# Attention steps that carry gate products: a reordering of a two-layer mixing kernel

## The chip, the cores and the metric

The kernel runs on one core of a Trainium2 chip. The metric is the device time of one execution in microseconds, lower is better. The time before is the median of three runs; one more execution was taken with the hardware profiler, and every row below is from that one.

## The reference, cut to what matters

Two layers of a backbone over 256 latent and 256 context tokens, width 1024. In the second layer only the latent tokens are carried to the end.

```python
for l in range(DEPTH):
    x, s = ffn_sublayer(x, ...), ffn_sublayer(s, ...)
    ...
    out_x, out_s, v_first = token_mixing(hx, hs, p, v_first, ..., not last)
    x = x + mod_x[:, :, 5] * out_x
    x = ffn_sublayer(x, ...)

def token_mixing(hx, hs, p, ...):
    cols_x, cols_s = split_cols(hx @ p['w_in'], IN_SPLITS), split_cols(hs @ p['w_in'], IN_SPLITS)
    ...
    ret_x  = retention_output(ox_f + flip_seq(ox_b), cols_x[3])
    att_x  = window_context_attention(aqx, akx, avx, aks, avs, sink)
    rwkv_x = rwkv_output(yx_f + yx_b, r_x, v_x, dirs_x, g_x, p)
    out_x  = branch_merge(ret_x, att_x, rwkv_x, cols_x[8], p)

def branch_merge(ret, att, rw, gate_logits, p):
    g_ret, g_att, g_rw = jnp.split(jax.nn.sigmoid(gate_logits), N_BRANCH, axis=-1)
    merged = g_ret * (ret @ p['w_ret']) + g_att * (att @ p['w_att']) + g_rw * (rw @ p['w_rwkv'])
    return merged @ p['w_out']
```

The gates are `cols_x[8]`: 3072 columns of the projection, 24 tiles of 128. They need nothing but the normed input, and nothing needs them before the branches are merged.

## The kernel before, in words

Activations lie with features on the partitions and the 512 tokens (context, then latent) along a row. A weight block is 128x128; four of them come in one DMA (`raw`, queue SP), ScalarE casts them to a high part (`whi`, line 114) and VectorE makes the rest (`wlo`, line 115). A product of a block with a tile of activations is three matmuls (`mm3`, lines 186 to 188). `dense` (line 330) does one output tile of 128 columns: eight blocks, 24 matmuls, 512 wide in layer 0 and 256 wide in layer 1, where only the latent half is wanted.

`mix` (its loop stands near the end of the listing) runs the token mixing of a layer as a list of pieces named in `ORDER` (line 55), one string for each layer:

- `lo`, `c0` to `c3`: the projections of the third branch (RWKV-7), four head pairs.
- `A`p and `C`p: `rw_front` of pair p for the context half (`A`) and the latent half (`C`). It ends in matmuls at line 976, in VectorE work on their results, in a trip through DRAM, and in a triangular solve on GpSimd, 31 rounds of two operations (lines 1008 and 1009), whose result goes to DRAM (`td`).
- `B`p and `D`p: `rw_back` of the same. `rw_merge` loads the solve's result (`z`), copies it on ScalarE (line 1026) and transposes it on VectorE (lines 1023 and 1027), and uses it in small matmuls (lines 1035 and 1040). `rw_chain` then walks four chunks in two directions; each step is a chain of matmul 1079/1081, ScalarE 1083, matmul 1086, ScalarE 1088, matmul 1090, VectorE 1102, and on to the next 1079/1081. `rw_out` closes it (1131, 1134).
- `P`, `H`: projections and heads of the retention branch. `kv`, `q0`, `q1`: keys, values and queries of attention.
- `t0` to `t3`: `att_pair`, two heads of attention each, over blocks of 128 queries (four steps in layer 0, two in layer 1). A step has for each of its two heads the scores (lines 757, 758, 761, one PSUM bank `ps_sc`), the maximum on VectorE (764), the exponential on ScalarE (767), transposes on TensorE (773), a copy on ScalarE (774) and the products with the values (776).
- `G0` to `G11`: `gates`, two gate tiles each: `dense`, a tanh on ScalarE (line 589), a store to DRAM.

After the list, `branches` projects and merges the three branches with the stored gates. The list is the order of tracing, not the order on the engines: the program is scheduled by the framework with a timeline of its own, which lets a later piece fill the waits of an earlier one, within the buffers that are free. `plan_mix` (line 58) packs the weights in the order of the list.

Of the kernel before, what the change touches and what calls it, by code (L numbers as in the profile page):

```python
# [51 lines left out]

ORDER = ['lo c0 A0 C0 B0 P0 kv c1 D0 H0 H1 q0 A1 t0 P1 t1 G0 C1 B1 H2 G1 c2 H3 G2 D1 A2 G3 q1 B2 P2 G4 C2 H4 t2 G5 t3 c3 A3 G6 H5 D2 G7 G8 P3 H6 G9 C3 B3 H7 D3 G10 G11', 'lo c0 A0 C0 P0 H0 kv B0 D0 c1 A1 H1 q0 t0 G0 t1 C1 G1 B1 P1 c2 D1 H2 A2 H3 P2 C2 G2 G3 H4 G4 c3 q1 G5 t2 t3 G6 B2 H5 D2 G7 A3 C3 G8 P3 B3 G9 G10 H6 H7 D3 G11']


def plan_mix(l):
    r0 = RCOL // 128
    out = []  # L60
    for w in ORDER[l].split():
        k, j = w[0], w[1:]
        if w == "lo":
            out.append(("lo", [("mix", kt, r0 + 12 + j) for kt in range(KT) for j in range(3)]))
            if l > 0:
                out.append(("vd", [("vd", 0, 0), ("vd", 0, 1)]))
        elif k == "c":
            p = int(j)
            out += [(f"r{p}", fm("mix", r0 + p)), (f"k{p}", fm("mix", r0 + 4 + p)), (f"v{p}", fm("mix", r0 + 8 + p))]
        elif k == "P":  # L70
            p = int(j)
            out += [(f"rq{p}", fm("mix", p)), (f"rk{p}", fm("mix", 4 + p)), (f"rv{p}", grp("mix", 8 + 2 * p))]
        elif k == "H":
            out.append((f"rg{j}", fm("mix", 16 + int(j))))
        elif w == "kv":
            out.append(("akv", grp("mix", 28)))
        elif k == "q":
            out.append((f"aq{j}", grp("mix", 24 + 2 * int(j))))
        elif k == "G":
            out += [(f"g{g}", fm("mix", 45 + g)) for g in range(2 * int(j), 2 * int(j) + 2)]  # L80
    for n in range(KT):
        out.append((f"ba{n}", fm("watt", n, 4)))
    out += [(f"br{n}", fm("wret", n)) for n in range(KT)]
    out += [(f"bw{n}", fm("wrw", n, 4)) for n in range(KT)]
    out += [(f"wo{n}", fm("wout", n)) for n in range(KT)]
    return out
# [36 lines left out]
def body(nc, tc, I, O, es, dbg=None):  # L123
# [61 lines left out]
    def mm3(o, w, h, start, stop):  # L185
        PE.matmul(o, w[0], h[0], start=start, stop=False)  # L186
        PE.matmul(o, w[0], h[1], start=False, stop=False)  # L187
        PE.matmul(o, w[1], h[0], start=False, stop=stop)  # L188

    def rsqrt(y, x):  # L190
        p, n = x.shape
# [138 lines left out]
    def dense(W, key, H, c, o):  # L330
        bl = W.take(key)
        for j, t in enumerate(bl):
            mm3(o[:, c], W.get(t), hl(H[j], c), j == 0, j == len(bl) - 1)

    def last_out(W, key, H, gate):

# [243 lines left out]
        SP.dma_start(out=st["od"][8 + h, :, c], in_=g[:, c])  # L580


    def gates(W, H, j, S, st):
        c = span(S)
        for g in range(2 * j, 2 * j + 2):
            o = ps("mm")
            dense(W, f"g{g}", H, c, o)
            t = ft()
            A.activation(t[:, c], o[:, c], AF.Tanh, scale=0.5)
            SP.dma_start(out=st["gd"][g, :, c], in_=t[:, c])  # L590

    def spilled(st, j, n, S, dst, mark, scale=None):
        c = span(S)
# [145 lines left out]
                    V.tensor_sub(qT[pr][h][ot, CS[half]], pt[hs, pr * 256:pr * 256 + 256], qT[pr][h][hs, CS[half]].bitcast(F32))  # L739
        st["qT", 2 * grp_], st["qT", 2 * grp_ + 1] = qT  # L740

    def att_pair(pj, S, st):
        c = span(S)
        q = st["qT", pj]
        (kd, kl), v = st["kT"], st["v"]
        t0 = c.start // 128
        po = ps("po")
        nm, es, sum_ = (sm(8, k, 4).rearrange("p (t h) -> p t h", h=2) for k in ("anm", "aes", "asum"))
        for qt in range(t0, 4):
            qs = slice(qt * 128, qt * 128 + 128)  # L750
            n = 256 if qt < 2 else 512
            nk = n // 128
            sc, p = [], []
            for hh in range(2):
                sc.append(ps("sc")[:, 0:n])
                p.append(mk([128, 512], "ae", 4)[:, 0:n])
                PE.matmul(sc[hh], q[hh][:, qs], kd[hh][:, 0:n], start=True, stop=False)
                PE.matmul(sc[hh], q[hh][:, qs], kl[hh][:, 0:n], start=False, stop=(qt < 2))
                if qt >= 2:
                    far = 5 - qt  # L760
                    PE.matmul(sc[hh][:, 256 + (far - 2) * 128:256 + (far - 2) * 128 + 128], st["aeye"], st["amask"][:, qt - 2], start=False, stop=True)
            mx = sm(2, "amx", 16)
            for hh in range(2):
                V.tensor_reduce(mx[:, hh:hh + 1], sc[hh], axis=AX.X, op=ALU.max)
                V.scalar_tensor_tensor(nm[:, qt, hh:hh + 1], mx[:, hh:hh + 1], -1.0, st["nsink"][:, 2 * pj + hh:2 * pj + hh + 1], ALU.mult, ALU.min)
            for hh in range(2):
                A.activation(p[hh], sc[hh], AF.Exp, bias=nm[:, qt, hh:hh + 1], accum_out=sum_[:, qt, hh:hh + 1])
            for hh in range(2):
                if hh == 0 or n == 512:
                    pt, pT = ps("ap"), mk([128, 512], "aT", 2)  # L770
                w0 = hh * 256 if n == 256 else 0
                for j in range(nk):
                    PE.transpose(pt[:, w0 + j * 128:w0 + j * 128 + 128], p[hh][:, j * 128:j * 128 + 128], ident)
                A.copy(pT[:, w0:w0 + n], pt[:, w0:w0 + n])
                for j in range(nk):
                    PE.matmul(po[:, qt * 128 + hh * 64:qt * 128 + hh * 64 + 64], pT[:, w0 + j * 128:w0 + j * 128 + 128], v[:, j * 128 + hh * 64:j * 128 + hh * 64 + 64], start=(j == 0), stop=(j == nk - 1))
        nt = slice(t0, 4)
        V.tensor_tensor(es[:, nt], nm[:, nt], st["sink"][:, 2 * pj:2 * pj + 2].unsqueeze(1).to_broadcast([128, 4 - t0, 2]), ALU.add)
        A.activation(es[:, nt], es[:, nt], AF.Exp)
        V.tensor_tensor(sum_[:, nt], sum_[:, nt], es[:, nt], ALU.add)  # L780
        V.reciprocal(sum_[:, nt], sum_[:, nt])
        y, t = mk([128, 512], "ae", 4), mk([128, 512], "aT", 2)
        V.tensor_tensor(y[:, c].rearrange("p (u d) -> p u d", d=64), po[:, c].rearrange("p (u d) -> p u d", d=64),
                        sum_[:, nt].rearrange("p t h -> p (t h)").unsqueeze(2).to_broadcast([128, 2 * (4 - t0), 64]), ALU.mult)
        yt = ps("ap")
        for qt in range(t0, 4):
            PE.transpose(yt[:, qt * 128:qt * 128 + 128], y[:, qt * 128:qt * 128 + 128], ident)
        A.copy(t[:, c], yt[:, c])
        SP.dma_start(out=st["od"][4 + pj, :, c], in_=t[:, c])
# [386 lines left out]
    def mix(l, W, H, S, vf, mark, st):  # L1176
# [4 lines left out]
        for w in ORDER[l].split():  # L1181
# [15 lines left out]
            elif k == "q":  # L1197
                att_q(W, H, int(j), S, st)
            elif k == "t":
                att_pair(int(j), S, st)  # L1200
            elif k == "G":
                gates(W, H, int(j), S, st)
        return branches(W, S, st), st["mark"]

    def mix_out(l, W, ms, S, xd):
# [161 lines left out]
```

## Time and profile before

| | |
|---|---|
| median of 3 runs | 2948.22 us (2942.67 to 2951.27) |
| the profiled execution's own time | 2950.47 us |
| its span in the profile | 2948.7 us |
| TensorE (PE) busy | 2797.0 us, 95% |
| VectorE (DVE) busy | 2002.5 us, 68% |
| ScalarE (ACT) busy | 1319.8 us, 45% |
| GpSimd (POOL) busy | 376.2 us, 13% |
| mean granted clock of TensorE | 0.963 |

The mixing of layer 0 takes the stretch from about 410 to 1314 us, that of layer 1 from about 2070 to 2747 us; the rest is feed-forward, which the change does not touch. Matmuls overlap in the records, so a matmul's own duration is longer than the time it adds; the time it adds is read from one start to the next. [...] In the timeline a bracket holds the idle time of that engine just before the row and what ended it.

### The profile page before, as it was taken

The page shows a single profiled execution, that of the slowest core. Times are in us where ns is not written, and L with a number is a line of the kernel's source. Part 1 is how long each engine was busy: PE and PEld are TensorE (multiplying, and loading weights), DVE is VectorE, ACT ScalarE, POOL GpSimd, SP SyncE. Part 2 cuts the span into 40 slices and gives each one's busy share as a digit, 9 for nine tenths or more (in the row PEclk, how much of TensorE's full clock was granted, in tenths as well). Part 3 has the DMA queues.
Part 4 walks back from the last instruction along what each step waited for, and adds up shares of the span by engine and source line. Part 5 has one row for each costly group of instructions (what it writes and reads, how often), then busy time and mean ns, then how long its engine had stood idle before and what let it go on. Part 6 is the DMA issues. An engine that isn't in the chain of part 4 may idle for free. (4 is left out here: it accounts for less than half of the span.)

```text
span 2948.7 us, 47410 instructions
## 1 busy us (share of the span) xinstructions
PE 2797.0 (95%) x16761; PEld 2389.1 (81%) x16761; DVE 2002.5 (68%) x4677; ACT 1319.8 (45%) x2968; POOL 376.2 (13%) x1068
## 2 busy tenths in 40 slices
PE   7999999889999999999999999999989889899999
PEld 6888888767877787788888888888878788788999
DVE  7977668676676666566756466465787767678655
ACT  3322245556555654333223232233567665565544
POOL 0000000522132112000000000000033434330000
PEclk9999999789999999999999999999999888899999
DMA  7655534212333136534534435343433234246554
GB/s 267 232 189 183 163 122 130 83 39 82 111 97 89 49 123 207 176 102 147 195 114 169 147 111 185 104 164 122 137 90 108 75 110 116 61 124 212 170 179 154
DMA packets 259727, 400.97 MB, mean 136 GB/s; under 512 B 78752, under 2 KB 96288, under 8 KB 259488
## 3 DMA queue, kind: packets, MB, share of 16 engines
q1 hardware_dynamic: 259488, 397.93, 42.2%
q8 instruction: 132, 2.16, 0.3%
q14 instruction: 107, 0.88, 0.1%
HBM read 368.33 MB, written 25.82 MB: 134 GB/s over the span
## 5 line engine op out<-in xcount | busy, mean ns | idle before, releaser
L114 ACT CAST whi<-raw 128x512 fp32r<-128x512 f32 x954 | 564.1, 618 | 675.7 <-PE ps_mm L187 350.0
L186 PE MATMUL ps_mm<-hall,whi 128*128 128x512 f32 (+1 forms) x2320 | 845.1, 365 | 10.2 <-DVE rr_v L801 4.0
L188 PE MATMUL ps_mm<-hall,wlo 128*128 128x512 f32 (+1 forms) x2320 | 842.6, 364 | 2.0 <-DVE wlo L115 2.0
L187 PE MATMUL ps_mm<-hall,whi 128*128 128x512 f32 (+1 forms) x2320 | 840.8, 363 | 0.0
L115 DVE TENSOR_TENSOR wlo<-raw,whi 128x512 fp32r<-128x512 f32 x954 | 643.8, 691 | 104.3 <-ACT whi L114 68.3
L186 PEld LDWEIGHTS ps_mm<-hall,whi 128*128 128x128 f32 x2320 | 442.9, 191 | 80.6 <-ACT cst L981 4.4
L188 PEld LDWEIGHTS ps_mm<-hall,wlo 128*128 128x128 f32 x2320 | 441.6, 191 | 74.8 <-DVE wlo L115 4.1
L187 PEld LDWEIGHTS ps_mm<-hall,whi 128*128 128x128 f32 x2320 | 442.0, 191 | 71.4 <-issue 0.2
L186 PE MATMUL ps_mm<-hid,whi 128*128 128x512 f32 (+1 forms) x737 | 260.6, 354 | 0.0
L187 PE MATMUL ps_mm<-hid,whi 128*128 128x512 f32 (+1 forms) x737 | 259.9, 354 | 0.0
L188 PE MATMUL ps_mm<-hid,wlo 128*128 128x512 f32 (+1 forms) x737 | 257.3, 354 | 0.0
L1008 POOL TENSOR_TENSOR cst<-acc,cst 128x60 f32<-128x60 f32 (+24 forms) x496 | 172.4, 348 | 615.5 <-DMA acc<-ad__10934 59.2
L401 DVE TENSOR_TENSOR ft<-ft,ps_mm 128x512 f32<-128x512 f32 (+1 forms) x80 | 49.7, 621 | 210.4 <-PE ps_mm L188 198.1
L373 DVE SCALAR_TENSOR_TENSOR x<-ps_mm,cst,x 128x256 f32<-128x256 f32 x136 | 61.0, 480 | 193.1 <-PE ps_mm L188 193.1
L853 POOL TENSOR_TENSOR ll<-lora,lh 128x512 fp32r<-128x512 f32 x8 | 10.3, 1282 | 1359.2 <-DVE ft L300 942.6
L1009 POOL TENSOR_TENSOR cst<-cst 128x60 f32<-128x60 f32 (+24 forms) x496 | 176.2, 355 | 38.1
L236 DVE SCALAR_TENSOR_TENSOR ft<-m,cd 128x1024 bf16<-128x1024 f32 x136 | 163.0, 1221 | 9.8 <-DMA m<-ada 9.8
L237 DVE SCALAR_TENSOR_TENSOR m<-m,cd 128x1024 f32<-128x1024 f32 x136 | 165.4, 1221 | 0.7
L186 PEld LDWEIGHTS ps_mm<-hid,whi 128*128 128x128 f32 x737 | 139.1, 189 | 19.6
L187 PEld LDWEIGHTS ps_mm<-hid,whi 128*128 128x128 f32 x737 | 139.1, 189 | 19.4
L188 PEld LDWEIGHTS ps_mm<-hid,wlo 128*128 128x128 f32 x737 | 138.5, 189 | 19.4
L187 PE MATMUL ps_mm<-wlo,hall 128*128 128x256 f32 x416 | 122.6, 295 | 2.7 <-DVE wlo L115 2.6
(339 smaller groups left out, 4505.3 us busy)
## 6 DMA issues: line engine op xcount, KB each, us to landing
m<-ada SPq DMA_DIRECT2D x136, 512.0 KB, 4.4
raw<-w0b SPq DMA_DIRECT2D x214, 256.0 KB, 2.9
raw<-w1b SPq DMA_DIRECT2D x211, 256.0 KB, 3.2
raw<-w0a SPq DMA_DIRECT2D x132, 256.0 KB, 2.8
raw<-w0c SPq DMA_DIRECT2D x132, 256.0 KB, 4.5
raw<-w1a SPq DMA_DIRECT2D x132, 256.0 KB, 4.3
raw<-w1c SPq DMA_DIRECT2D x132, 256.0 KB, 3.9
gd<-ft SPq DMA_DIRECT2D x24, 256.0 KB, 2.0
```

Of the source, the lines that this page charges most:

```text
L114: nc.scalar.copy(hi, raw)
L115: nc.vector.tensor_sub(lo, raw, hi.bitcast(F32))
L186: PE.matmul(o, w[0], h[0], start=start, stop=False)
L187: PE.matmul(o, w[0], h[1], start=False, stop=False)
L188: PE.matmul(o, w[1], h[0], start=False, stop=stop)
L236: V.scalar_tensor_tensor(junk, raw, 1.0, st["cond"][0], ALU.mult, ALU.mult, accum_out=md[:, kt, 0:1])
L237: V.scalar_tensor_tensor(raw, raw, 1.0, st["cond"][1], ALU.mult, ALU.mult, accum_out=md[:, kt, 1:2])
L373: V.scalar_tensor_tensor(xs[n][:, CS[s]], o[:, CS[s]], gate[:, n, s:s + 1], xs[n][:, CS[s]], ALU.mult, ALU.add)
L401: V.tensor_tensor(sg[:, c], sg[:, c], pu[:, c], ALU.mult)
L853: G.tensor_sub(ll, lw, lh.bitcast(F32))
L1008: G.tensor_tensor(w, acc[j // 16][:, j % 16, j + 1:32].unsqueeze(1).to_broadcast([128, m, n]), tt[:, 0:m, j:j + 1].to_broadcast([128, m, n ...
L1009: G.tensor_tensor(tt[:, 0:m, j + 1:32], tt[:, 0:m, j + 1:32], w, ALU.add)
```

## The change

In the list the pieces `G0` to `G7` are gone from both layers, and `P`, `q1`, `t` and their neighbours stand closer or in another order; `G8` to `G11`, the last eight gate tiles, are kept at their places. The sixteen other gate tiles are done inside attention: pair j computes gates 4j to 4j+3, one in each step in layer 0 and two in each step in layer 1, traced after the step's exponentials. Two orders are forced on TensorE (`issue_after` adds an order on the engine of the instruction, not a wait on a semaphore): the gate's matmuls come after the last score matmul of the step, and the step's transposes come after the gate's last matmul. `mm3` and `dense` return their last instruction for this. The program has the same instructions on every engine as before, in another order.

```diff
@@ -52,7 +52,7 @@
 
 
 
-ORDER = ['lo c0 A0 C0 B0 P0 kv c1 D0 H0 H1 q0 A1 t0 P1 t1 G0 C1 B1 H2 G1 c2 H3 G2 D1 A2 G3 q1 B2 P2 G4 C2 H4 t2 G5 t3 c3 A3 G6 H5 D2 G7 G8 P3 H6 G9 C3 B3 H7 D3 G10 G11', 'lo c0 A0 C0 P0 H0 kv B0 D0 c1 A1 H1 q0 t0 G0 t1 C1 G1 B1 P1 c2 D1 H2 A2 H3 P2 C2 G2 G3 H4 G4 c3 q1 G5 t2 t3 G6 B2 H5 D2 G7 A3 C3 G8 P3 B3 G9 G10 H6 H7 D3 G11']
+ORDER = ['lo c0 A0 C0 B0 P0 kv c1 D0 H0 H1 q0 A1 t0 P1 C1 t1 B1 H2 c2 H3 D1 A2 q1 B2 t2 P2 C2 H4 c3 t3 A3 H5 D2 G8 P3 H6 G9 C3 B3 H7 D3 G10 G11', 'lo c0 A0 C0 P0 H0 kv B0 D0 c1 A1 H1 q0 t0 C1 t1 B1 P1 c2 D1 H2 A2 H3 P2 C2 H4 c3 q1 t2 B2 t3 H5 D2 A3 C3 G8 P3 B3 G9 G10 H6 H7 D3 G11']
 
 
 def plan_mix(l):
@@ -76,8 +76,9 @@
             out.append(("akv", grp("mix", 28)))
         elif k == "q":
             out.append((f"aq{j}", grp("mix", 24 + 2 * int(j))))
-        elif k == "G":
-            out += [(f"g{g}", fm("mix", 45 + g)) for g in range(2 * int(j), 2 * int(j) + 2)]
+        elif k in "Gt":
+            n = 2 if k == "G" else 4
+            out += [(f"g{g}", fm("mix", 45 + g)) for g in range(n * int(j), n * int(j) + n)]
     for n in range(KT):
         out.append((f"ba{n}", fm("watt", n, 4)))
     out += [(f"br{n}", fm("wret", n)) for n in range(KT)]
@@ -185,7 +186,7 @@
     def mm3(o, w, h, start, stop):
         PE.matmul(o, w[0], h[0], start=start, stop=False)
         PE.matmul(o, w[0], h[1], start=False, stop=False)
-        PE.matmul(o, w[1], h[0], start=False, stop=stop)
+        return PE.matmul(o, w[1], h[0], start=False, stop=stop).ins
 
     def rsqrt(y, x):
         p, n = x.shape
@@ -330,7 +331,8 @@
     def dense(W, key, H, c, o):
         bl = W.take(key)
         for j, t in enumerate(bl):
-            mm3(o[:, c], W.get(t), hl(H[j], c), j == 0, j == len(bl) - 1)
+            ins = mm3(o[:, c], W.get(t), hl(H[j], c), j == 0, j == len(bl) - 1)
+        return ins
 
     def last_out(W, key, H, gate):
 
@@ -580,14 +582,15 @@
         SP.dma_start(out=st["od"][8 + h, :, c], in_=g[:, c])
 
 
-    def gates(W, H, j, S, st):
+    def gates(W, H, gs, S, st):
         c = span(S)
-        for g in range(2 * j, 2 * j + 2):
+        for g in gs:
             o = ps("mm")
-            dense(W, f"g{g}", H, c, o)
+            ins = dense(W, f"g{g}", H, c, o)
             t = ft()
             A.activation(t[:, c], o[:, c], AF.Tanh, scale=0.5)
             SP.dma_start(out=st["gd"][g, :, c], in_=t[:, c])
+        return ins
 
     def spilled(st, j, n, S, dst, mark, scale=None):
         c = span(S)
@@ -739,7 +742,7 @@
                     V.tensor_sub(qT[pr][h][ot, CS[half]], pt[hs, pr * 256:pr * 256 + 256], qT[pr][h][hs, CS[half]].bitcast(F32))
         st["qT", 2 * grp_], st["qT", 2 * grp_ + 1] = qT
 
-    def att_pair(pj, S, st):
+    def att_pair(W, H, pj, S, st):
         c = span(S)
         q = st["qT", pj]
         (kd, kl), v = st["kT"], st["v"]
@@ -755,22 +758,27 @@
                 sc.append(ps("sc")[:, 0:n])
                 p.append(mk([128, 512], "ae", 4)[:, 0:n])
                 PE.matmul(sc[hh], q[hh][:, qs], kd[hh][:, 0:n], start=True, stop=False)
-                PE.matmul(sc[hh], q[hh][:, qs], kl[hh][:, 0:n], start=False, stop=(qt < 2))
+                mark = PE.matmul(sc[hh], q[hh][:, qs], kl[hh][:, 0:n], start=False, stop=(qt < 2)).ins
                 if qt >= 2:
                     far = 5 - qt
-                    PE.matmul(sc[hh][:, 256 + (far - 2) * 128:256 + (far - 2) * 128 + 128], st["aeye"], st["amask"][:, qt - 2], start=False, stop=True)
+                    mark = PE.matmul(sc[hh][:, 256 + (far - 2) * 128:256 + (far - 2) * 128 + 128], st["aeye"], st["amask"][:, qt - 2], start=False, stop=True).ins
             mx = sm(2, "amx", 16)
             for hh in range(2):
                 V.tensor_reduce(mx[:, hh:hh + 1], sc[hh], axis=AX.X, op=ALU.max)
                 V.scalar_tensor_tensor(nm[:, qt, hh:hh + 1], mx[:, hh:hh + 1], -1.0, st["nsink"][:, 2 * pj + hh:2 * pj + hh + 1], ALU.mult, ALU.min)
             for hh in range(2):
                 A.activation(p[hh], sc[hh], AF.Exp, bias=nm[:, qt, hh:hh + 1], accum_out=sum_[:, qt, hh:hh + 1])
+
+            ng = 4 // (4 - t0)
+            with tc.issue_after(mark):
+                mark = gates(W, H, range(4 * pj + (qt - t0) * ng, 4 * pj + (qt - t0 + 1) * ng), S, st)
             for hh in range(2):
                 if hh == 0 or n == 512:
                     pt, pT = ps("ap"), mk([128, 512], "aT", 2)
                 w0 = hh * 256 if n == 256 else 0
                 for j in range(nk):
-                    PE.transpose(pt[:, w0 + j * 128:w0 + j * 128 + 128], p[hh][:, j * 128:j * 128 + 128], ident)
+                    with tc.issue_after(mark):
+                        PE.transpose(pt[:, w0 + j * 128:w0 + j * 128 + 128], p[hh][:, j * 128:j * 128 + 128], ident)
                 A.copy(pT[:, w0:w0 + n], pt[:, w0:w0 + n])
                 for j in range(nk):
                     PE.matmul(po[:, qt * 128 + hh * 64:qt * 128 + hh * 64 + 64], pT[:, w0 + j * 128:w0 + j * 128 + 128], v[:, j * 128 + hh * 64:j * 128 + hh * 64 + 64], start=(j == 0), stop=(j == nk - 1))
@@ -1197,9 +1205,9 @@
             elif k == "q":
                 att_q(W, H, int(j), S, st)
             elif k == "t":
-                att_pair(int(j), S, st)
+                att_pair(W, H, int(j), S, st)
             elif k == "G":
-                gates(W, H, int(j), S, st)
+                gates(W, H, range(2 * int(j), 2 * int(j) + 2), S, st)
         return branches(W, S, st), st["mark"]
 
     def mix_out(l, W, ms, S, xd):
```

What the scheduler made of it is shown at three places. Lines of the changed kernel are numbered a few higher: 186 to 188 became 187 to 189, 757/758/761 became 760/761/764, 773 became 781, 774 became 782, 776 became 784, 589 became 591, and the lines of the RWKV branch moved by 8 (1026 became 1034, 1079 became 1087).

**TensorE, layer 0, one step of pair 1 (`t1`).** Before, transposes of one head, then the next head's scores, then other pieces' small matmuls, then the product with the values:

```order
L773 MATMUL ps_ap<-cst,ae 128x128 x4
L757 MATMUL ps_sc<-kd,qT 128x512
L758 MATMUL ps_sc<-kl,qT 128x512
L761 LDWEIGHTS pa
L761 MATMUL ps_sc<-pa 128x128
L1052 MATMUL ps_rx<-cst,rr_v 128x128 x2
L1040 MATMUL ps_rx<-tg,rb 32x32 x9
L776 MATMUL ps_po<-kv,aT 128x64 x4
```

In the changed program, a step of pair 1:

```order
L781 MATMUL ps_ap<-cst,ae 128x128 x4
L1094 MATMUL ps_rx<-cst,tg 64x64 x4
L760 MATMUL ps_sc<-kd,qT 128x512
L761 MATMUL ps_sc<-kl,qT 128x512
L764 LDWEIGHTS pa
L764 MATMUL ps_sc<-pa 128x128
L187 MATMUL ps_mm<-hall,whi 128x512
L188 MATMUL ps_mm<-hall,whi 128x512
L189 MATMUL ps_mm<-hall,wlo 128x512
```

The last three rows begin a gate. Fifteen more of its matmuls follow before the product 784 that needs the transposes 781 of the first row, and the transposes of the scores shown here come only after the gate's last matmul. Before, 14 matmuls stood between such transposes and their product, all but two of them small.

**ScalarE, layer 1, the copies of `z` that belong to `D0` (line 1026, now 1034).** Before:

```order
L912 ACTIVATE rt<-rt 128x512
L114 CAST whi<-raw 128x512
L767 ACTIVATE ae,cst<-ps_sc,cst 128x512
L1026 COPY tg<-z 32x8x32 x2
L1088 COPY ve<-ps_rx 64x128
L920 ACTIVATE rt<-rt 128x512
L921 ACTIVATE rt<-rt 128x512
L941 ACTIVATE rt<-rt,cst 128x512
L472 COPY ft<-ps_mm 128x512
```

In the changed program:

```order
L782 COPY aT<-ps_ap 128x512
L980 COPY arz<-ar 64x2x64 x4
L1034 COPY tg<-z 32x8x32
L115 CAST whi<-raw 128x512
L1034 COPY tg<-z 32x8x32
L115 CAST whi<-raw 128x512
L966 ACTIVATE kbT<-ps_rf,cst 128x512
L770 ACTIVATE ae,cst<-ps_sc,cst 128x512
L591 ACTIVATE ft<-ps_mm 128x256
L787 ACTIVATE cst<-cst 128x4
L115 CAST whi<-raw 128x512 x2
```

Behind the copies of `z` stood work of `B0`, `A1` and `P1` before. Now two weight casts (115) stand there, one of them between the two copies, then an exponential of attention (770), a gate's tanh (591) and two more casts: the gate tiles of `t0` and `t1` have moved in front of the projections of `P1`.

**TensorE, layer 0, the last chain (`D3`).** Before, projections of the branches (`ps_mm`) stand between the chain's steps, and only its last 28 matmuls follow each other without one:

```order
L188 MATMUL ps_mm<-hall,wlo 128x512
L186 MATMUL ps_mm<-hall,whi 128x512
L1090 MATMUL ps_rx<-ve,kbT 128x128
L187 MATMUL ps_mm<-hall,whi 128x512
L188 MATMUL ps_mm<-hall,wlo 128x512
L186 MATMUL ps_mm<-hall,whi 128x512
L187 MATMUL ps_mm<-hall,whi 128x512
L188 MATMUL ps_mm<-hall,wlo 128x512
L186 MATMUL ps_mm<-hall,whi 128x512
L1090 MATMUL ps_rx<-ve,kbT 128x128
```

In the changed program the chain's last 55 matmuls follow each other, of which these are eight rows:

```order
L1098 MATMUL ps_rx<-ve,kbT 128x128
L1087 MATMUL ps_rx<-cst,gk 128x128
L1089 MATMUL ps_rx<-cst,ar 128x128
L1115 MATMUL ps_rx<-ve,tg 64x64 x2
L1094 MATMUL ps_rx<-cst,tg 64x64 x2
L1087 MATMUL ps_rx<-cst,gk 128x128
L1089 MATMUL ps_rx<-cst,ar 128x128
L1098 MATMUL ps_rx<-ve,kbT 128x128
```

The branch projections that stood between them are used up earlier, beside `B3`. In layer 1 the same bare run at the end of `D3` grows from 12 to 38 matmuls.

## Rows read from the trace of the kernel before

**Rows 1.** The page, head and part 1: busy us, share, instructions.
```profile
span 2948.7 us, 47410 instructions
PE 2797.0 (95%) x16761; PEld 2389.1 (81%) x16761; DVE 2002.5 (68%) x4677; ACT 1319.8 (45%) x2968; POOL 376.2 (13%) x1068
```

**Rows 2.** Timeline of PE: start us, us, instruction; a 512-wide and a 256-wide product.
```profile
2318.96 0.40 PE L186 MATMUL ps_mm<-hall,whi 128*128 128x512 f32 x1
2319.20 0.39 PE L187 MATMUL ps_mm<-hall,whi 128*128 128x512 f32 x1
...
2503.06 0.28 PE L187 MATMUL ps_mm<-hall,whi 128*128 128x256 f32 x1
2503.18 0.28 PE L188 MATMUL ps_mm<-hall,wlo 128*128 128x256 f32 x1
```

**Rows 3.** Waits of PE, 577 to 1265 us: us in total, times, longest.
```profile
PE ps_po L776 <- ACT aT L774: 4.1, 5, 1.6
...
PE ps_ap L773 <- ACT ae L767: 1.6, 2, 0.9
```

**Rows 4.** Waits of PE, 2200 to 2724 us.
```profile
PE ps_po L776 <- ACT aT L774: 2.1, 2, 1.6
```

**Rows 5.** Windows, layer 1: each from a pair's last matmul 976 to its merge.
```profile
2154.00:2197.00 43.00, 37.63 (x244) 33.54 (x242) 38.67 (x114) 25.58 (x55) 24.83 (x66) 0.96 0.39 111
2207.00:2253.00 46.00, 45.46 (x313) 39.01 (x312) 33.59 (x108) 29.09 (x74) 23.47 (x66) 0.94 0.38 105
2286.00:2335.00 49.00, 37.62 (x220) 31.65 (x219) 38.56 (x111) 27.61 (x69) 21.41 (x67) 0.79 0.26 66
...
2409.00:2463.00 54.00, 48.68 (x295) 41.62 (x294) 39.16 (x110) 29.66 (x73) 22.39 (x66) 0.84 0.35 99
2474.00:2534.00 60.00, 50.25 (x350) 42.66 (x349) 36.79 (x111) 36.45 (x97) 24.95 (x66) 0.86 0.31 84
2607.00:2652.00 45.00, 42.37 (x367) 36.96 (x365) 31.21 (x87) 27.74 (x79) 22.51 (x62) 1.00 0.41 115
```

**Rows 6.** Timeline, layer 1: last matmuls 976, first uses of the solve, and one stall.
```profile
2286.64 0.39 PE L976 MATMUL ps_rf<-arz,kb 128*128 128x128 f32 x2
...
2326.36 0.40 ACT L1026 COPY tg<-z 32x256 f32<-32x256 f32 x1 [1.50 <-DMA z<-td]
...
2473.77 1.03 PE L976 MATMUL ps_rf<-arz,kb 128*128 128x256 f32 x4
...
2516.52 0.43 DVE L1023 STREAM_TRANSPOSE rb<-z 32x256 f32<-32x256 f32 x1 [7.35 <-DMA z<-td]
...
2516.52 0.40 ACT L1026 COPY tg<-z 32x256 f32<-32x256 f32 x1 [4.73 <-DMA z<-td]
...
2518.47 0.66 PE L1079 MATMUL ps_rx<-cst,gk 128*64 128x128 f32 x2 [5.79 <-DVE cst L1102]
```

**Rows 7.** Windows: attention steps, two VectorE peaks, a bare chain.
```profile
700.00:730.00 30.00, 27.17 (x212) 21.36 (x213) 19.13 (x59) 20.66 (x62) 4.06 (x16) 0.89 0.20 56
...
840.00:860.00 20.00, 19.81 (x152) 17.83 (x151) 19.08 (x42) 11.49 (x25) 14.04 (x31) 1.00 0.55 164
...
980.00:1020.00 40.00, 36.97 (x264) 29.86 (x262) 26.90 (x82) 26.92 (x76) 0.08 (x1) 0.87 0.15 42
...
1222.00:1232.00 10.00, 8.02 (x64) 6.03 (x62) 5.64 (x17) 2.75 (x9) 0.00 (x0) 1.00 0.16 52
...
2300.00:2320.00 20.00, 14.40 (x67) 11.71 (x68) 18.59 (x60) 11.15 (x25) 16.08 (x51) 0.66 0.12 34
...
2500.00:2540.00 40.00, 31.19 (x243) 25.02 (x241) 17.18 (x53) 24.19 (x68) 9.47 (x31) 0.79 0.11 27
```

## Prediction

> **What bounds the kernel now.** I read the head of the page first: TensorE (PE) is busy 95% of the span, the next engine, VectorE (DVE), 68% [rows 1]. So the time is PE's work plus what PE loses, and since the change has the same instructions on every engine, only the losses can move. There are two kinds: PE idle, and PE at the lower clock. Feed-forward loses little and is not touched. The loss lies in the two mixing stretches, and I asked three views for it.
>
> The waits view of PE gives what attention itself costs. The reader should see how small it is: in layer 0 PE waited 4.1 us for the copy behind the transposes and 1.6 us for the exponentials [rows 3], in layer 1 2.1 us [rows 4]. The scheduler already fills attention's waits with other pieces.
>
> The windows view shows what costs more. In layer 1 six windows run from a pair's last matmul 976 to the first use of its solve [rows 5]. The solve is a fixed path through DVE, DRAM, GpSimd and DRAM again, and the timeline gives its length: 2286.64 to 2326.36 is 39.7 us, 2473.77 to 2516.52 is 42.8 us [rows 6]; I use 42. Each of these windows lasts 43 to 60 us, and PE is idle 0.5 to 11.4 us of it.
>
> The clock column is the third: 0.79 to 0.89 in windows with attention in them [rows 7] and 0.79 in 2286 to 2335 [rows 5], where PE had idled just before.
>
> **The change part by part.** Prices first. A 512-wide matmul adds 0.24 us and a 256-wide one 0.12 us from start to start [rows 2], so a gate tile of 24 matmuls is 5.8 us of PE in layer 0 and 2.9 us in layer 1. It is moved with everything it issues: two DMAs, two casts, two subtractions, a tanh, a store. Those counts do not change, and no queue gets more of them; I cost them at nothing, because DMA is idle more than half of every window [rows 5]. Without that cover the price is a weight that comes late, a rival below.
>
> *Attention's own waits.* Every step now has at least 5.8 us of gates between scores and transposes, against softmax waits of at most 1.6 us [rows 3]. The 4.1 + 1.6 + 2.1 = 7.8 us go: **-7.8**. Lower bound of the gain 0, if the copies are late for another reason.
>
> *The merge `B1` in layer 1.* In the old order I count 24 wide, 24 narrow and 105 small matmuls between the last 976 of `A1` and the first 1035 of `B1`: 5.8 + 2.9 + 18.9 (an estimate: 0.18 us each, the mean of their start-to-start times there) = 28 us of work, for a path of 42. That window lost 49.0 - 37.6 = 11.4 us of idle time [rows 5]. In the new order the `t1` gates and `P1` stand there: 71 wide, 216 narrow, 118 small, 64 us. The solve is then ready before PE comes to it: **-11.4**, between 0 (DVE, busy 38.6 of the 49 us, still holds PE) and all of it. I take all, since the work now exceeds the path by half.
>
> *The merges `D0`, `B2` and `D3` in layer 1.* Here the change takes work away. `D0`: 40 us become 28 (148 narrow, 24 wide and 90 small become 95 narrow and 94 small). `B2`: 39 become 33. `D3`: 40 become 37. The path of 42 does not shrink. For `D0` the window was 46 us [rows 5], 6 more than its work; now it is at least 42, so it loses at least 14, which is 8 more, and 14 more if its other losses stay on top. I take 10. `B2` (54 us for 39) and `D3` (45 for 40) need lose no more than they do, and at most 6 and 5 more; I take 2 together, near the floor, since both windows already exceed the path. **+12**, between +8 and +25. Two other merges keep theirs: `B0` stands as it was, and `D2` keeps 40 us of work and its stall of 5.8 us [rows 6]. In layer 0 `B1` to `D3` had 43 to 73 us and get 61 to 81, so nothing waits there.
>
> *Who is queued behind an early merge.* The stall of 2518.47 shows it: ScalarE and DVE stood still 4.7 and 7.4 us for `z` of `D2`, and a chain of `B2` behind them, which had its data, cost PE 5.8 us [rows 6]. [...]
>
> *Bare chains.* `D3` ends with 55 instead of 28 matmuls without cover in layer 0 and 38 instead of 12 in layer 1, 53 more. The bare 28 of the old order lost 10.0 - 8.0 = 2.0 us [rows 7], so 53 lose **+3.8**. Upper bound twice that, at the lower clock.
>
> *A DVE peak.* In layer 0 the gates that stood beside `B1` and `D1` are gone, and `q1`, `A2`, `B1` and `D1` crowd together; all but the gates are heavy on DVE. The nearest rows are two windows with DVE at 19.1 and 18.6 of 20 us: the first cost PE 0.2 us, the second 5.6 [rows 7]. The middle: **+2.8**.
>
> *Clock.* In 700 to 730, 980 to 1020, 2500 to 2540 [rows 7] and 2286 to 2335 [rows 5] the low clock can cost at most 0.11 x 30 + 0.13 x 40 + 0.21 x 40 + 0.21 x 49 = 27 us; part of it fell on time in which PE waited anyway, so I take half back, 13.6. Three new thin places (`D0` in layer 1, the DVE peak, the bare `D3`) cost as much as the smallest of these, 3.3 each: 9.9. **-3.7**, between -27 and +10.
>
> Sum: -7.8 - 11.4 + 12 + 3.8 + 2.8 - 3.7 = **-4.3 us**. The profiled execution took 2950.5 us, so 2946.2 for it; it stood 2.3 above the median of 2948.2, and against that median I predict **2944 us**. A measurement of this kernel can tell about 0.3%, 9 us, from no change: under 2939 is faster, over 2957 slower.
>
> **The rivals.**
> - *The early merges block two queues* (slower). `D0`, `B2` and `D3` of layer 1 reach their copies before the solve has landed, ScalarE and DVE stop, and the gates' weight casts stop with them. For it: the stall of 5.8 us [rows 6], and the two casts behind `D0`'s copies. Against: `B0`, with 34 us of work for the same path, lost only 43.0 - 37.6 = 5.4 us [rows 5]. All three at their upper bounds give +25 instead of +12, and without the gates' cover some 5 of the 7.8 us stay: -4.3 + 13 + 5 = +14, **2962 us**. It decides once ScalarE waits more than some 5 us for `z` of `D0`.
> - *The clock comes back whole* (faster). With gates among the thin steps PE no longer idles before these stretches, and the new thin places don't bring the clock down. For it: 2300 to 2320 has the most idle time and the lowest clock, 0.66 [rows 7]. Against: PE's thin work, RWKV's chains, remains. It adds -13.4 and drops the 9.9: -4.3 - 23.3 = -28, **2920 us**.
> - *It only trades one filler for another.* Attention was filled already (7.8 us in all), and each gate that fills attention leaves a gap of its own size; 0 us, **2948 us**.
>
> **How the numbers follow.** Forecast 0.46, with 2934 to 2954 as its own range: of that about 0.14 lies under 2939, 0.29 within 0.3%, 0.03 above. The blocked queues 0.22, the clock 0.22, the mere trade 0.10. So faster 0.14 + 0.22 = 0.36, the same 0.29 + 0.10 = 0.39, slower 0.03 + 0.22 = 0.25. The range takes in most of both outer cases and the bounds of the unknown terms that pull the same way: 2914 to 2966.
>
> **What would show it.** Right: the waits for 774 and 767 fall from 7.8 us to under 2; the window before `B1` in layer 1 has under 4 us of idle PE; the window before `D0` there lasts 42 to 48 us with over 6 idle; ScalarE waits there for `z`; the end of `D3` in layer 0 shows idle of some 4 us. Wrong: attention's waits stay, or the low clock moves by more than 15 us in sum, or a stall over 8 us appears at a place that I have not named, a late weight above all.

## The result, and the profile after

The changed kernel takes **2974.98 us** (median of 4 runs, 2973.76 to 2979.05) against 2948.77 (4 runs, 2942.67 to 2951.27): a ratio of **1.0094, 95% interval 1.0076 to 1.0113**, 26 us slower. The prediction was 2944, with 2914 to 2966 as its range.

The head of the page, to be read beside [rows 1]:

```profile
span 2971.9 us, 47395 instructions
PE 2819.0 (95%) x16761; PEld 2405.3 (81%) x16761; DVE 1998.8 (67%) x4677; ACT 1316.0 (44%) x2968; POOL 371.6 (13%) x1068
```

Each engine has the same number of instructions (the totals differ by 15 semaphore instructions), and PE is busy 22 us longer. So by the records the loss is not idle time: the matmuls themselves took longer. The mean granted clock, which was 0.963, says why:

```profile
core 0: 2971.9 us, clock 0.953
```

The clock has two levels in these two profiles, 1.00 and 0.50: windows of 1 us of the changed kernel read 1.00 at 2217, 0.63 at 2218, where it falls, and 0.50 from 2219 to 2245. Twice what is missing to 1.000, times the span, is then the time at 0.50: some 218 us before and 279 us after, about 60 more. At 0.50 a 512-wide product adds 0.43 us from start to start (1249.81 to 1250.24 us of the changed kernel) where it adds 0.24 at 1.00 [rows 2], so of 60 us up to some 27 are lost where PE has no slack.

Where it went is read best at equal work. For each matmul I take the start-to-start time that its kind needs with full cover (the lower quartile over the profile of before), add these up, and compare when two programs have done the same sum. A program may do other pieces first, so a single point can mislead; steps that stay count. In us against the profile of before, at ten of its times (the named runs follow below):

| time in before | 784 | 852 | 914 | 1217 | 1242 | 2066 | 2223 | 2610 | 2686 | 2735 |
|---|---|---|---|---|---|---|---|---|---|---|
| changed kernel | 2 | 25 | 8 | 12 | 19 | 19 | 26 | 9 | 20 | 24 |
| layer0_only | 2 | 25 | 8 | 13 | 22 | 21 | 20 | 7 | 9 | 10 |
| p2_early | 5 | 11 | 14 | 17 | 28 | 29 | 36 | 12 | 25 | 24 |
| late_gates | 0 | 24 | 7 | 20 | 20 | 21 | 28 | 12 | 22 | 24 |
| no_forced_order | -16 | 2 | -11 | 13 | 23 | 24 | 29 | 4 | 15 | 14 |
| free_gate | -17 | -2 | -16 | -2 | 11 | 12 | 11 | -19 | -5 | -4 |
| before_hold6 | -3 | -3 | -5 | 7 | 2 | 1 | 2 | -5 | -2 | -9 |

The changed kernel falls back by 23 us between 784 and 852 us, gets 17 back by 914 (the old kernel has a loss of its own there: PE is busy 32.2 of the 40 us from 860 to 900), and falls back by 7 at the end of layer 0. In layer 1 it falls back at 2223 and at the end. Layer 1 of the profiled execution of before was a poor one: two other runs with the old layer 1 (layer0_only, before_hold6) gain 10 to 11 us on it there. Each row is one execution, so a few us in it are chance.

**The first place: layer 0, 790 to 850 us.** The windows view, before and after (a stretch and its length, busy time and number of instructions on PE, weight loads, DVE, ACT and POOL, then the granted clock, the busy share of the DMA engines and GB/s; [rows 5, 7] have the same columns):

```profile
790.00:850.00 60.00, 59.44 (x429) 50.76 (x428) 46.88 (x134) 36.58 (x88) 6.59 (x15) 1.00 0.36 110
```
```profile
820.00:830.00 10.00, 4.27 (x15) 3.34 (x16) 9.44 (x39) 3.48 (x7) 0.00 (x0) 0.61 0.22 73
...
790.00:850.00 60.00, 49.82 (x351) 42.50 (x350) 46.21 (x157) 29.66 (x80) 1.82 (x4) 0.83 0.20 64
```

DVE does the same amount in both, 46 to 47 of 60 us. Before, PE had other work meanwhile; now it is idle for 10 us and its clock is 0.83 in place of 1.00. The timeline of PE after shows what it waits for:

```profile
818.86 0.28 PE L189 MATMUL ps_mm<-whi,hall 128*128 128x256 f32 x1
824.49 2.18 PE L965 MATMUL ps_rf<-cst,kb 128*128 128x128 f32 x8 [5.35 <-DVE kb L954]
827.91 1.11 PE L575 MATMUL ps_po<-cst,ft 128*128 128x128 f32 x4 [1.24 <-DVE ft L571]
828.82 1.91 PE L984 MATMUL ps_rf<-arz,kb 128*128 128x256 f32 x4
832.17 0.69 PE L1142 MATMUL ps_rx<-cst,rb 64*128 64x64 f32 x4 [1.44 <-DVE rb L1139]
```

The last weight product (a matmul into `ps_mm`, lines 187 to 189) of `q1` is at 818.86; then `A2` waits on DVE, and for 27 us there is no weight product, until the first gate of `t2` starts at 846.00, right behind the scores that it must follow (845.88).

**The second place: layer 1, the chain of `B0`.** Its window up to the merge is as it was (43 us, 37.10 busy, against the first of [rows 5]). Behind the merge, up to the pair's first scores, in the windows view of before and then of after:

```profile
2198.00:2230.00 32.00, 30.29 (x237) 25.65 (x235) 25.10 (x85) 21.39 (x65) 12.97 (x32) 0.84 0.46 135
```
```profile
2217.00:2243.00 26.00, 26.00 (x151) 18.77 (x151) 19.14 (x76) 16.05 (x54) 7.80 (x25) 0.52 0.25 68
```

In the changed kernel there is no idle time at all in the records, and all but about 1 us runs at a clock of 0.50. The timeline there, eight of its rows:

```profile
2216.88 0.59 PE L1043 MATMUL ps_rx<-rb,cst 32*32 32x32 f32 x13 [2.27 <-DVE rb L1031]
...
2222.11 1.22 PE L561 MATMUL ps_po<-ft 128*128 128x128 f32 x4
2223.26 1.12 PE L1087 MATMUL ps_rx<-cst,gk 128*64 128x128 f32 x4
2224.33 0.69 PE L1094 MATMUL ps_rx<-cst,tg 64*64 64x64 f32 x4
2224.95 2.07 PE L984 MATMUL ps_rf<-arz,kb 128*128 128x256 f32 x4
...
2237.57 0.69 PE L1087 MATMUL ps_rx<-cst,gk 128*64 128x128 f32 x2
...
2242.52 0.77 PE L760 MATMUL ps_sc<-kd,qT 128*128 128x512 f32 x1
2243.10 0.63 PE L761 MATMUL ps_sc<-kl,qT 128*128 128x512 f32 x1
```

For 25.6 us there is not one weight product, and the next ones in the list are the gates of `t0`, which must come after its scores. Before, the four gate tiles of `G0` and `G1` ran in this stretch, ahead of the scores (their tanh at 2217 to 2231 us, the first scores at 2229.5).

**The waits that the change was to fill.** PE's waits after, layer 0 and then layer 1, beside [rows 3, 4]:

```profile
PE ps_rf L965 <- DVE kb L954: 8.7, 3, 5.4
...
PE ps_po L784 <- ACT aT L782: 1.5, 1, 1.5
```
```profile
PE ps_po L784 <- ACT aT L782: 2.9, 2, 2.6
```

The copy's waits fell from 4.1 to 1.5 us in layer 0 and rose from 2.1 to 2.9 in layer 1; that of line 773 is gone. That is 3.4 of 7.8 us, and the waits of 965 (957 before) for DVE's 954, which had been 1.0 us, alone cost 7.7 us more, over twice that.

### The profile page after: what moved, and what is told of

Same layout as the page of the kernel before. It is cut to its first block, busy times and chain, and to the rows that moved or that the text cites. A ratio compares the mean times of both kernels' runs of the same rounds, so it can differ in the third digit from the quotient of the medians.

```text
span 2971.9 us, 47395 instructions
## 1 busy us (share of the span) xinstructions
PE 2819.0 (95%) x16761; PEld 2405.3 (81%) x16761; DVE 1998.8 (67%) x4677; ACT 1316.0 (44%) x2968; POOL 371.6 (13%) x1068
## 4 chain that ended last, share of the span: by engine, by line
PE 50%; POOL 5%; DVE 3%; DMA 2%; issue 2%; ACT 1%; SPq 1%; POOLq 0%; DVEq 0%; ACTq 0%
PE ps_mm L187 13%; PE ps_mm L189 13%; PE ps_mm L188 13%; POOL cst L1017 2%; POOL cst L1016 2%; PE ps_mm L366 1%; PE ps_rx L1094 1%; PE ps_rf L984 1%; DMA z<-td 1%; PE ps_rx L366 1%; PE ps_rx L1087 1%; SPq L1020 0%; PE ps_rx L1115 0%; DVE wlo L116 0%; DVE ft L301 0%
## 5 line engine op out<-in xcount | busy, mean ns | idle before, releaser
L1016 POOL TENSOR_TENSOR cst<-acc,cst 128x60 f32<-128x60 f32 (+24 forms) x496 | 166.1, 335 | 648.5 <-DMA acc<-ad__10934 53.8
L187 PE MATMUL ps_mm<-whi,hall 128*128 128x256 f32 x416 | 120.7, 291 | 2.8 <-DVE ft L526 1.3
```

Source lines behind the costliest of these rows:

```text
L1016: G.tensor_tensor(w, acc[j // 16][:, j % 16, j + 1:32].unsqueeze(1).to_broadcast([128, m, n]), tt[:, 0:m, j:j + 1].to_broadcast([128, m, n ...
```

## The experiments

My first theory was that a gate spent inside attention is missing later: at the VectorE-heavy stretch around `A2`, and as cover of `D3`, the last chain. Rivals: the two forced orders, the new order of the neighbours, and layer 1's early merges. `u`j in a list stands for an attention pair without gates.

**layer0_only**: layer 1 as before.

```diff
-ORDER = [changed layer 0, changed layer 1]
+ORDER = [changed layer 0, 'lo c0 A0 C0 P0 H0 kv B0 D0 c1 A1 H1 q0 u0 G0 u1 C1 G1 B1 ... D3 G11']
```

> Layer 0 as in the changed kernel, layer 1 as before. By work done, the trace of the changed kernel falls back by 21 us in layer 0 and by 3 us in layer 1. If the loss lies in layer 0 (gates spent before the VectorE peak at 780 to 860 us and before the last chain): +19 to +23 us, about 2970. If it is spread over both layers in proportion to their attention: +10 to +14, about 2961. If layer 1's early merges make it: within 5 us of 2949.

Measured: 2961.5 us, ratio 1.0055 (1.0033 to 1.0077). About 14 of the 26 us come with layer 0 and the rest with layer 1. In the trace layer 0 loses what it lost in the changed kernel (the table), so the trace's split of 21 to 3 was wrong: the old layer 1 that it was compared with was a poor execution.

**gates_back**: the changed order of the neighbours, `G0` to `G7` as pieces again.

```diff
-... t0 P1 C1 t1 B1 H2 c2 H3 D1 A2 q1 B2 t2 P2 C2 H4 c3 t3 A3 H5 D2 ...
+... u0 P1 C1 u1 G0 B1 H2 G1 c2 H3 G2 D1 A2 G3 q1 B2 u2 P2 G4 C2 H4 G5 c3 u3 A3 G6 H5 D2 G7 ...
```

> The changed order of the other pieces in both layers, but the gates G0 to G7 as pieces of their own again beside the neighbours that they had, and nothing forced in attention's steps. If the place of the gates makes the loss: back to before, 2943 to 2955. If the new order of the neighbours makes it (C1 ahead of t1, t2 ahead of P2, c3 ahead of t3; B2 ahead of t3 in layer 1): it stays at 2968 to 2980.

Measured: 2943.7 us, 0.9990 (0.9975 to 1.0005). The new order of the neighbours costs nothing.

**old_neighbours**: the reverse, gates in the steps and the neighbours of before.

```diff
-... t0 P1 C1 t1 B1 ... q1 B2 t2 P2 C2 H4 c3 t3 A3 H5 ...
+... t0 P1 t1 C1 B1 ... q1 B2 P2 C2 H4 t2 t3 c3 A3 H5 ...
```

> The gates in attention's steps, with the two forced orders, but the other pieces in the order of before. If the place of the gates makes the loss: 2965 to 2985, as the changed kernel or a little worse. If the new order of the neighbours makes it: 2943 to 2955.

Measured: 2973.3 us, 1.0084 (1.0053 to 1.0116): all of the loss. It is the gates in the steps.

**no_forced_order**: both `issue_after` blocks taken away.

> The changed kernel without the two forced orders on TensorE; the gates are traced at the same places. If spending the gates early makes the loss: still 2965 to 2985, with idle time at the VectorE peak and a bare last chain. If holding the transposes back behind a whole gate makes it: 2945 to 2955.

Measured: 2959.1 us, 1.0040 (1.0023 to 1.0057), between the two. By the table layer 0 is 16 us ahead of before at 784 and 11 at 914 us. It falls back by 34 us from there to 1242, about half of it at a last chain with no weight product from its merge to its end, 96 matmuls. Windows of that end:

```profile
1220.00:1230.00 10.00, 4.06 (x41) 3.27 (x42) 5.97 (x19) 1.55 (x3) 0.00 (x0) 0.61 0.42 131
1230.00:1240.00 10.00, 9.50 (x81) 7.92 (x80) 3.06 (x10) 5.10 (x18) 0.00 (x0) 0.71 0.01 2
1240.00:1250.00 10.00, 9.32 (x54) 7.65 (x52) 4.52 (x16) 2.49 (x10) 0.00 (x0) 0.63 0.00 0
```

So the forced orders cost something, and a bare chain does. This loss has another form than that of the changed kernel: in the profile PE is busy 2797.6 us at a mean clock of 0.963, both as before, and the span is 14 us longer, so it is idle time. The next four runs try bare chains and local mends.

**before_hold6**: the old kernel with a barer end.

```diff
-            a, mark = gated(..., st["step"] if n >= KT - 2 else None)
+            a, mark = gated(..., st["step"] if n >= KT - 6 else None)
```

> The kernel before, with six instead of two of the retention tiles of branches held behind the last step of D3, and nothing else. In the order on TensorE only the end of D3 changes: the matmuls that follow each other without cover at its end go from 28 to 45 in layer 0 and from 12 to 22 in layer 1, 27 more. By the price of the prediction (idle time alone, 0.07 us each): +2 us, not to be told from before. By the step found in the changed kernel's trace, some 0.33 us of lost time for each bare matmul: +9 us, 2952 to 2962.

Measured: 2942.7 us, 0.9994 (0.9981 to 1.0006): no slower, so the price of 0.33 us fails as a price of the whole. The trace tells what it missed. At the end of `D3` in layer 0 it does lose (from -4 at 1195 us to 7 at 1217, and 5 come back by 1242, since the held tiles follow without a gap). In layer 1 the held tiles cover the kernel's own last wait. First the end of layer 1's branches in before, then here, one execution of each:

```profile
2710.00:2725.00 15.00, 12.87 (x90) 12.30 (x91) 12.47 (x31) 7.83 (x17) 0.00 (x0) 0.89 0.51 162
```
```profile
2700.00:2716.00 16.00, 16.00 (x136) 16.00 (x135) 14.38 (x34) 8.42 (x18) 0.00 (x0) 1.00 0.75 230
```

A tile taken from one thin place is not lost if it fills another.

**p2_early**: `P2` stands at the VectorE-heavy stretch.

```diff
-... H3 D1 A2 q1 B2 t2 P2 C2 ...
+... H3 D1 P2 A2 q1 B2 t2 C2 ...
```

> The changed kernel with P2 moved in layer 0 from behind t2 to the place ahead of A2 and q1, so that 22 us of projections, with little for VectorE, stand at the VectorE peak. If the missing cover there costs for good what the trace shows at the place (some 20 us between 780 and 860 us): 2955 to 2963. If the peak only brings forward a loss that the kernel before has a little later (its window from 860 to 900 us), so that most comes back: 2968 to 2978.

Measured: 2972.8 us, 1.0086 (1.0067 to 1.0105). The gap at 852 us shrinks from 25 to 11, and by 914 the kernel is further behind than the changed one. The loss moves on.

**late_gates**: the gates of `t3` in layer 0 behind `D3`.

```diff
-... c3 t3 A3 ... H7 D3 G10 G11
+... c3 u3 A3 ... H7 D3 G6 G7 G10 G11
```

> The changed kernel, but in layer 0 the four gates of t3 are pieces of their own behind D3, and t3 has none in its steps. The bare end of D3 falls from 55 to 40 matmuls. If spending the gates early is what costs, by 0.33 us for each bare matmul: 5 us less, and 2966 to 2972; t3's own waits cost at most 3 back. If the gates' place in the list doesn't matter for the end: 2973 to 2978.

Measured: 2973.1 us, 1.0099 (1.0078 to 1.0120). The end of layer 0 no longer loses (20 at 1217, 20 at 1242), and what was saved there was lost before it. The first theory, in the form that the last chain wants the gates, falls: mending the end alone gives nothing.

**nf_late_gb**: an attempt at a better kernel, layer 0 as in late_gates without forced orders, layer 1 as in gates_back.

> An attempt at a better kernel: layer 0 as changed but without the forced orders and with t3's gates behind D3 (bare end 48 instead of 96 matmuls), layer 1 with the changed neighbours and the gates as pieces at their old places. By work done, layer 0 without forced orders was 12 us ahead of before until 1100 us and lost 26 us at its bare end; half of that stays: about +1 for layer 0, and -10 for layer 1 as in the run with the gates back. 2932 to 2946; if the gain until 1100 us was chance, 2945 to 2955.

Measured: 2952.9 us, 1.0025 (1.0014 to 1.0036): slower than before.

Both local mends of the changed kernel gave their time back elsewhere. What was left were the forced orders, one by one, and the clock.

**free_gate**: the first forced order away, the second kept.

```diff
-            with tc.issue_after(mark):
-                mark = gates(W, H, range(...), S, st)
+            mark = gates(W, H, range(...), S, st)
```

> The changed kernel without the first forced order alone: a gate's matmuls need no longer come after the step's last score, while the transposes still come after the gate. If what costs is that a gate, which needs nothing but the normed input, can no longer fill the thin stretches ahead of the scores: most of what taking both orders away gave comes back, 2955 to 2966. If it is the transposes held behind the gate: 2970 to 2980.

Measured: **2950.4 us, 1.0005 (0.9994 to 1.0017)**. Without this one edge all but 1.4 of the 26 us are gone (by the interval the kernel is 2 us faster to 5 us slower than before), more than I expected. The tanh behind each gate (line 591) shows where the gates went. The first two of `t0` in layer 1 and of `t2` in layer 0, in the changed kernel, then here:

```profile
2251.99 0.39 ACT L591 ACTIVATE ft<-ps_mm 128x256 f32<-128x256 f32 x1
2256.66 0.38 ACT L591 ACTIVATE ft<-ps_mm 128x256 f32<-128x256 f32 x1
...
853.22 0.60 ACT L591 ACTIVATE ft<-ps_mm 128x512 f32<-128x512 f32 x1
869.02 0.60 ACT L591 ACTIVATE ft<-ps_mm 128x512 f32<-128x512 f32 x1
```
```profile
2227.54 0.37 ACT L591 ACTIVATE ft<-ps_mm 128x256 f32<-128x256 f32 x1
2231.23 0.39 ACT L591 ACTIVATE ft<-ps_mm 128x256 f32<-128x256 f32 x1 [1.11 <-DVE ft L702]
...
828.21 0.60 ACT L591 ACTIVATE ft<-ps_mm 128x512 f32<-128x512 f32 x1
837.00 0.60 ACT L591 ACTIVATE ft<-ps_mm 128x512 f32<-128x512 f32 x1
```

They run 24 to 32 us earlier: ahead of the first scores of their steps (2239.0 us for both of `t0`, 830.9 and 845.2 us for those of `t2`; in the changed kernel the first scores, 2242.5 and 840.9 us, come before the tanh), in the chain of `B0` and in the VectorE-heavy stretch. The timeline of PE in the chain of `B0` in this run, then windows of it and of 790 to 850 us, and last the same window of the chain in the changed kernel:

```profile
2220.40 0.43 PE L1087 MATMUL ps_rx<-cst,gk 128*64 128x128 f32 x2
2221.16 0.39 PE L187 MATMUL ps_mm<-hall,whi 128*128 128x256 f32 x1 [0.32 <-DVE ft L580]
...
2224.03 0.28 PE L189 MATMUL ps_mm<-hall,wlo 128*128 128x256 f32 x1
2224.14 0.39 PE L1098 MATMUL ps_rx<-ve,kbT 128*128 128x128 f32 x2
```
```profile
2205.00:2243.00 38.00, 34.20 (x287) 29.36 (x286) 29.58 (x96) 24.34 (x70) 14.26 (x36) 0.96 0.48 137
```
```profile
790.00:850.00 60.00, 52.16 (x353) 43.93 (x352) 46.57 (x151) 34.80 (x94) 0.90 (x3) 0.91 0.28 88
```
```profile
2205.00:2243.00 38.00, 35.73 (x227) 28.08 (x226) 26.34 (x91) 21.55 (x66) 11.57 (x38) 0.67 0.27 68
```

A whole gate tile (24 products, 2221.16 to 2224.03) stands between two links of the chain, and the 38 us have a clock of 0.96 where the changed kernel has 0.67. The VectorE-heavy stretch is mended only in part: PE still has 7.8 us of idle time in 790 to 850. By the table, of the 28 us between this run and the changed kernel at 2735, 8 are there at the end of layer 0, 15 by 2223 (with the chain of `B0`) and all by 2610. So the two places hold about half of it; what the gates cover between 2223 and 2610 is not shown here. That the order costs the time is shown by the run, whatever the places.

**free_transposes**: the second forced order away, the first kept.

```diff
-                    with tc.issue_after(mark):
-                        PE.transpose(pt[...], p[hh][...], ident)
+                    PE.transpose(pt[...], p[hh][...], ident)
```

> The changed kernel without the second forced order alone: the transposes need no longer wait for the gate, the gate still comes after the scores. If the gate tied behind the scores is what costs: 2970 to 2980, as the changed kernel. If the transposes held behind the gate are: 2955 to 2966.

Measured: 2969.0 us, 1.0067 (1.0049 to 1.0085), just under its band: some 6 us came back, with the gates still tied, and its interval overlaps that of the changed kernel, so these 6 us are not clear of the noise. It is the first order, not the second. The other runs agree: those that keep the first order in both layers measure 2969 to 2975, those without it 2944 to 2959, and layer0_only, which keeps it in one, 2961.5. Why both away (2959) is worse than the first alone (2950) stays open. The bare 96 matmuls at the end of layer 0 are not the reason: in free_gate some 92 follow each other there too, from 1212.38 to 1239.82. By the table 10 of the 18 us between the two profiles come between 914 and 1217 us.

**filled_chains**: useless products in three chains.

```diff
+                if (l, p, s) == (1, 0, 0) or (p, s) == (3, 1):
+                    PE.matmul(x[:, 256:512], kbT[d][:, q], vb[:, 0:2]..., start=True, stop=True)
                 rr = sm(128, "rr", 2)[0:64]
...
+                (the same once more ahead of the copy into ve)
```

> The changed kernel with work that nothing needs: in every step of three chains (B0 of layer 1, D3 of both layers) two more 256-wide products, written to a part of the bank that the chain overwrites later; 48 in all, about 0.25 us each, 12 us of PE time if none of it falls into waits. If the lower clock over thin chain work is what costs: the stretch of B0 in layer 1, now 26 us at a granted clock of 0.50 (2217 to 2243), rises above 0.75 and gets shorter by 5 us or more in spite of 4 us of added work, and the whole is no slower than the changed kernel, 2962 to 2976. If the clock only shows waits that would be there anyway: each place is longer by up to 4 us, and the whole 2977 to 2987.

Measured: 2974.5 us, 1.0086 (1.0067 to 1.0105): 48 products, some 12 us of work, cost nothing that can be told. Windows of the chain of `B0` in layer 1, of `D3` in layer 0 and of the products behind it:

```profile
2221.00:2246.00 25.00, 24.42 (x162) 17.34 (x162) 18.83 (x75) 15.66 (x51) 4.19 (x14) 0.80 0.26 77
1231.00:1254.00 23.00, 21.05 (x142) 15.42 (x141) 9.72 (x30) 6.41 (x21) 0.00 (x0) 1.00 0.10 39
1254.00:1264.00 10.00, 10.00 (x46) 8.07 (x45) 6.71 (x19) 2.39 (x4) 0.00 (x0) 1.00 0.00 0
```

In the changed kernel they were 0.52, 0.81 and 0.84:

```profile
1231.00:1249.00 18.00, 15.20 (x105) 12.23 (x106) 8.77 (x30) 5.77 (x20) 0.00 (x0) 0.81 0.09 34
...
1249.00:1259.00 10.00, 10.00 (x39) 7.71 (x39) 6.63 (x19) 1.77 (x3) 0.00 (x0) 0.84 0.00 0
```

The clock comes back with the products (mean 0.962 against 0.953) and pays for them. The stretch of `B0` got shorter by 1.4 us (2221.32 to 2245.57, against 2216.88 to 2242.52), not by the 5 expected, and the chain of `D3` longer by 4 (1231.34 to 1253.81, against 1230.26 to 1248.79 bare), so added work is only a break-even: what the chain lacks is useful work.

**mixed_order**: an attempt at a better kernel, layer 0 of before, layer 1 of gates_back.

> An attempt at a better kernel: layer 0 in the order of before, layer 1 with the changed neighbours and the gates as pieces at their old places, nothing forced. In the traces layer 1 gained 17 us in this order (run gates_back) and 7 to 11 us in the order of before in two other runs, so some 6 to 10 us over before can be left: 2936 to 2945. If the gain was chance: 2944 to 2952.

Measured: 2943.9 us, 0.9980 (0.9966 to 0.9995), with a clock of 0.970 in its profile, which is the fastest of its 12 executions (2932.9 us). That is 31 us under the changed kernel and 5 us or 0.2% under before: little beside the spread of the 23 executions of before (2938.6 to 2960.1 us), though the interval leaves out 1.

## Why the prediction was wrong

**The step that failed** is that the first forced order has no term in the sum: I read it as part of moving a tile and costed it at nothing. With it fell the clock term, -3.7 in the sum and +19 in the trace. Behind both stands the way of counting in "`B0` stands as it was". I counted what stands between a pair's last matmul 976 and its merge, where PE can be seen waiting, and found work for 42 us there; up to its merge `B0` did stand as it was. I did not count what stands in the chain that follows the merge. There PE shows no idle time, so the view of waits does not name it, but it runs thin matmuls (most of 2 to 128 columns) alone, at a mean clock of 0.52 in the chain of `B0`. The gates had filled these chains, and they could because they need nothing but the normed input. The forced order took that freedom away. free_gate shows its price: without it, and with the second order kept, 24.5 of the 26 us are gone.

By the terms:

- *Attention's own waits, -7.8*: measured -3.4. Right in kind, and half as large.
- *`B1` in layer 1, -11.4*: its window (line 3 of the fence below) has 7.4 us of idle PE against 11.4, so -4.0, a third; as a sign of being right I had named under 4 us idle.
- *`D0`, `B2`, `D3` in layer 1, +12*: right in size. The windows last 42, 50 and 46 us for 28, 33 and 37 us of work: 14, 17 and 9 us lost, against 6, 15 and 5 before, +14. But the loss of `D0` has another form. I expected over 6 us of idle PE and ScalarE waiting for `z`; PE is idle 1.4 us, ScalarE waits 1.9 us, and the clock is 0.77: the 28 us of work were stretched over the window.

```profile
2173.00:2216.00 43.00, 37.10 (x240) 33.62 (x240) 37.41 (x112) 25.41 (x54) 25.12 (x66) 0.96 0.41 111
2226.00:2268.00 42.00, 40.56 (x238) 32.21 (x237) 30.19 (x102) 25.60 (x69) 21.28 (x66) 0.77 0.28 73
2283.00:2361.00 78.00, 70.61 (x477) 62.47 (x475) 56.06 (x136) 42.63 (x100) 26.58 (x67) 0.91 0.41 115
...
2430.00:2480.00 50.00, 40.96 (x240) 33.24 (x239) 40.61 (x118) 26.77 (x68) 20.98 (x66) 0.87 0.30 77
...
2642.00:2688.00 46.00, 42.27 (x338) 37.43 (x338) 29.42 (x84) 25.64 (x78) 20.32 (x62) 0.85 0.40 111
```

- *Bare chains, +3.8*: too small. The bare 55 matmuls of layer 0 take from 1230.26 to 1248.79, 0.34 us each, and 15.2 of 18 us are busy by the records (the window above); I had priced the idle part alone, 0.07 each [rows 7]. The bare 28 of before had taken 0.30 us each (1222.94 to 1231.43), so the row that I used already held more than its idle time. At equal work the end of layer 0 lost 7 us. But before_hold6 shows that this isn't a price for the whole either.
- *The DVE peak, +2.8*: the place was right, the size wrong: 23 us at the spot, and 6 left by 914 us. I took the middle of two windows in which PE was busy 19.8 and 14.4 of 20 us [rows 7]; here it was busy 4.3 of 10.
- *Clock, -3.7*: the term with the wrong sign. I expected gates in thin steps to bring back half of 27 us and charged 3.3 us for each new thin place. The time at a clock of 0.50 went from some 218 to 279 us instead. The prediction had named more than 15 us as what would make it wrong. At equal work, counting as half-clock loss what matmuls in stretches at 0.50 took beyond their time at 1.00, this loss rose by 19 us and all others together by some 4. At their places the other five terms measure -3.4, -4, +14, +7 and +6, each worse than I had said; these hold the lower clock of their stretches too, so the two countings cannot be added. That the other losses come near my -0.6 in sum is in part luck.

Of the rivals none was it. The queues blocked by early merges were not: ScalarE's waits for `z` in layer 1 are 25.2 us against 21.4, and 1.9 at `D0`. There was little occasion for an early `D0` to hold the casts behind it: the merge came after the full path of 42 us, with ScalarE waiting those 1.9 us. The clock that comes back whole was the opposite of what happened, and "it only trades one filler for another" is true of the mends (p2_early, late_gates); of the change it is true in kind only, since the gaps that the gates left cost 26 us more than those that they filled.

## What to carry to other kernels

Work that depends on little was this scheduler's best filler, and an ordering edge that pins such work behind one consumer can cost what it filled elsewhere, so list every place where it runs now before pinning it. Count cover also where an engine is busy with thin work, not only where it waits: here the granted clock showed such a place (0.52 in the chain of `B0`), where the records of PE have no idle time. Judge a local mend by the end of the kernel, since two stretches were mended here and the loss moved on.

## What the runs showed of the hardware

In the changed kernel TensorE ran from 2217 to 2243 us with no idle time in its records, and all but about 1 us of it at a clock of 0.50 (0.52 in the mean), on matmuls of 2 to 128 columns and few wider ones (11 of 151). The ends of matmuls in the records are modelled, so gaps too short to show cannot be ruled out. With two useless 256-wide products in each step of the chain the same stretch was at 0.80 (filled_chains), with gate tiles in it at 0.96 (free_gate, over 38 us, against 0.67 over the same 38 us) and at 0.84 (before, over 32 us). PE had been idle for 2.27 us just before 2216.88, and the clock read 1.00 in the microsecond from 2217 and 0.50 from 2219 on. What brought it down is not shown; no idle time in the records kept it there.

That 48 useless products, some 12 us of work, cost nothing in the whole (2974.5 against 2975.0 us) was the other surprise; the time at a clock of 0.50, by the mean clocks (0.962 against 0.953), fell by some 50 us.
